# Two-layer hybrid decoder trunk: the opening's shift and scale columns side by side in one accumulator

## The chip, the cores and the metric
The kernel runs on one core of one Trainium2 chip. The metric is the device time of one execution in microseconds (us). Engines are named as in the profile: PE (TensorE, matrix products; PEld its weight loads), DVE (VectorE), ACT (ScalarE), POOL (GpSimd) and SP (SyncE, which issues most loads). Each engine works through its own list of instructions in order. SBUF is the on-chip memory, PSUM the eight banks that PE writes to.

## What is computed
Two decoder layers over 256 positions of width D = 2048 in float32. Each has a token mixer (layer 0 forgetting attention, layer 1 sliding-window attention) and a gated feed-forward network. Each of these four sub-layers is modulated by vectors made from one conditioning vector `c`:

```python
c_act = jax.nn.silu(c)
for i in range(DEPTH):
    mod = c_act @ ada_w[i] + ada_b[i]                 # ada_w[i]: 2048 x 12288
    sh1, sc1, g1, sh2, sc2, g2 = jnp.split(mod[:, None, :], 6, axis=-1)
    h = x * (1.0 + sc1) + sh1
    y = fox_attention(h, fox_w_in[j], ...)            # layer 0: proj = h @ w_in; layer 1: swa_attention
    x = layer_norm(DEEPNORM_ALPHA * x + (1.0 + g1) * y, ...)
    h = x * (1.0 + sc2) + sh2
    y = conv_ffn(h, ...)
    x = layer_norm(DEEPNORM_ALPHA * x + (1.0 + g2) * y, ...)
```

Nothing of layer 0 can start before `sh1` and `sc1` (the first 2 x 2048 columns of `ada_w[0]`, 33.6 MB) are at least partly known. The change concerns how these two vectors are made.

## The kernel before
Weights are used in two float32r halves: a load `w` (two blocks of 128 rows by 512 columns, 512 KB) is rounded by ACT to `wh` (L276, a cast) and DVE makes the residual `wl = w - wh` (L287). PE multiplies both with the modulated, transposed input `hHL` (`hH` high, `hL` low half). Matmuls into `ws` are query and key projections, into `xs` value projections.

The **opening** (`opening`, with `first_block` for the projections) works in eight chunks of 256 of the 2048 columns of `sh1` and `sc1`; the variable is `cb`, and the texts say chunk 0 to 7. For a chunk:

1. SP loads the `ada_w` columns into tiles `wo` (L531), each with 4 of the 16 blocks of 128 rows, for 256 columns of the shift (v = 0) or the scale (v = 1): 8 loads of 512 KB. All loads, `wo` and `w`, share ten buffers (`wp`); a load is issued when the tile that held its buffer has been used. Every second chunk also loads 512 columns of x (512 KB).
2. Each row block is multiplied by its constant of `c_act` (`cact`, one per partition) and summed in the accumulator `oacc`. Shift and scale have separate columns, and each has two accumulators for even and odd row blocks, so four per chunk. The first product of each goes to POOL (L541, a TENSOR_SCALAR), the others to DVE (L543, a SCALAR_TENSOR_TENSOR: multiply and add). In chunk 0, three of each eight row blocks go to PE instead (`cps<-cact,wo`).
3. PE sums over the partitions by a product with ones (`cps<-ones,oacc`, 8 matmuls). A float32 matmul shows as two records in the trace.
4. DVE adds the bias: `cv` (L573, one for shift, one for scale). PE transposes the chunk's part of x (`sm<-ident,x`, L469, 4 transposes in `mod_turn`). `mod_pair` makes `hHL` of it: ACT and DVE write one half each of `t` (L484, L485), ACT rounds it (L85), DVE subtracts (L86).

From chunk 1 on, six weight loads per chunk (two items of `plan`, each with query, key and value part) run through `first_block` between these steps, with the input columns that earlier chunks have finished. After a chunk pair, ACT scales its columns of x in place by a constant (L639, in `scaled`), which may not happen before x has been transposed. After the opening the rest of the projections, attention, and so on follow, with the weights streamed in the same way; there DVE makes the other modulation vectors in the same manner (L404, L406, 1024 columns at a time).

The program's text doesn't fix the order in which an engine's instructions stand: a scheduler orders them by its own estimate of when each can run, except those handed to `pin`, which stay in program order among themselves. Eight semaphores, used in turn, mark landed transfers of SP; a load is issued only when the load eight before it has landed.

Of the kernel before, what the change touches and what calls it, by code (L numbers as in the profile page):

```python
# [10 lines left out]
F32 = mybir.dt.float32  # L11
# [3 lines left out]
ALU = mybir.AluOpType  # L15
AX = mybir.AxisListType

P = 128
D = 2048
S = 256  # L20
NT = S // P
KC = D // P
# [19 lines left out]
def hybrid_trunk(ctx: ExitStack, tc: tile.TileContext, a: dict, out: bass.AP):  # L42
    nc = tc.nc
# [5 lines left out]
    cst = ctx.enter_context(tc.tile_pool(name="cst", bufs=1))  # L49
    wp = ctx.enter_context(tc.tile_pool(name="wp", bufs=10))  # L50
# [12 lines left out]
    def ttile(name="t"):  # L63
        return tp.tile([P, 2 * S], F32, tag="t", name=name)

    def bank(name="sm"):
        return psp.tile([P, 512], F32, tag="ps", name=name)
# [7 lines left out]
    def mm(o, lhsT, rhs, start=False, stop=False, **kw):  # L75
        return nc.tensor.matmul(o, lhsT, rhs, start=start, stop=stop, **kw)  # L76

    def pin(ins, on=True):

        if on:  # L80
            tc.keep_in_program_order(ins)

    def split(h, l, src):

        nc.scalar.copy(h, src)  # L85
        nc.vector.tensor_tensor(l, src, f32(h), op=ALU.subtract)  # L86
# [16 lines left out]
    ones = cst.tile([P, P], F32, name="ones")  # L103
# [19 lines left out]
    cact = cst.tile([P, KC], F32, name="cact")  # L123
# [3 lines left out]
    acol = cst.tile([P, DEPTH, NADA], F32, name="acol")  # L127
# [259 lines left out]
    cols = {}  # L387
# [74 lines left out]
    def mod_turn(k, n=1):  # L462

        ps = [bank() for _ in range(n)]
        os = []
        for j in range(2):
            o = ps[j % n][:, j // n * S:(j // n + 1) * S]
            for t in range(NT):
                nc.tensor.transpose(o[:, t * P:(t + 1) * P], x[:, t, (k + j) * P:(k + j + 1) * P], ident)  # L469
            os.append(o)  # L470
        return os

    def mod_pair(G, B, k, ps, fast=False):
        tmp = ttile()
        if fast:
            g, b = ([c[:, k + j:k + j + 1] for j in range(2)] for c in (G, B))
            o = [tmp[:, j * S:(j + 1) * S] for j in range(2)]
            high = lambda j: nc.scalar.activation(hH[:, k + j, :], ps[j], AF.Identity, bias=b[j], scale=g[j])
            whole = lambda j: pin(nc.vector.tensor_scalar(o[j], ps[j], g[j], b[j], op0=ALU.mult, op1=ALU.add))
            high(0), whole(1), high(1), whole(0)  # L480
            for j in range(2):
                pin(nc.vector.tensor_tensor(hL[:, k + j, :], o[j], f32(hH[:, k + j, :]), op=ALU.subtract))  # L482
            return
        nc.scalar.activation(tmp[:, :S], ps[0], AF.Identity, bias=B[:, k:k + 1], scale=G[:, k:k + 1])  # L484
        nc.vector.tensor_scalar(tmp[:, S:], ps[1], G[:, k + 1:k + 2], B[:, k + 1:k + 2],  # L485
                                op0=ALU.mult, op1=ALU.add)
        split(hH[:, k:k + 2, :], hL[:, k:k + 2, :], tmp.rearrange("p (j s) -> p j s", j=2))
# [6 lines left out]
    def warm(n):  # L494

        o = bank("warm").rearrange("p (a b) -> p a b", b=P)
        for _ in range(n):
            pin(mm(o, onesr, onesr.unsqueeze(1).broadcast_to([P, 4, P]), start=True, stop=True))
# [21 lines left out]
    def opening(plan, proj, also):  # L520

        CB = 2 * P
        QK = 1024 // CB
        for v in range(2):
            cols[0, v] = cst.tile([P, KC], F32, tag=f"cv{v}", name="cv")

        def sums(cb, v, acc, ps):
            pe = 8 - (3 if cb == 0 else 0)
            for kq in range(0, KC, QK):
                w = wp.tile([P, QK, CB], F32, tag="w", name="wo")  # L530
                nc.sync.dma_start(w, a["ada_w"][0, kq * P:(kq + QK) * P, v * D + cb * CB:v * D + (cb + 1) * CB]  # L531
                                  .rearrange("(k p) f -> p k f", p=P))
                for k in range(QK):
                    kc = kq + k
                    if kc % 8 >= pe:
                        for j in range(2):
                            c = 2 * v + j
                            mm(ps[:, c:c + 1], w[:, k, j * P:(j + 1) * P], cact[:, kc:kc + 1],
                               start=c == 0 and kc == pe, skip_group_check=True)
                    elif kc < 2:  # L540
                        nc.gpsimd.tensor_scalar_mul(acc[:, v, k % 2, :], w[:, k, :], cact[:, kc:kc + 1])  # L541
                    else:
                        nc.vector.scalar_tensor_tensor(acc[:, v, k % 2, :], w[:, k, :], cact[:, kc:kc + 1],  # L543
                                                       acc[:, v, k % 2, :], op0=ALU.mult, op1=ALU.add)
                yield

        accs = cst.tile([P, D], F32, tag="acc", name="oacc").rearrange("p (c v q f) -> p c v q f", c=2, v=2, q=2)
        for cb, items in enumerate(plan):
            k = 2 * cb
            todo = [(*it, part) for it in items for part in range(3)]  # L550
            n = len(todo)
            if cb == D // CB:
                for it in todo:
                    proj(*it)
                break
            acc = accs[:, cb % 2]
            ps = bank("cps")
            also.get(cb, lambda: None)()
            steps = [g for v in range(2) for g in [sums(cb, v, acc, ps)] * (KC // QK)]
            for i, g in enumerate(steps):  # L560
                if i == 0 and cb % 2 == 0:
                    c = slice(cb * CB, (cb + 2) * CB)
                    nc.sync.dma_start(x[:, :, c], a["x"][0][:, c].rearrange("(t p) d -> p t d", p=P))
                next(g)
                while todo and n - len(todo) < (i + 1) * n // len(steps):
                    proj(*todo.pop(0))
            for c in range(4):
                for q in range(2):
                    mm(ps[:, c:c + 1], acc[:, c // 2, q, c % 2 * P:(c % 2 + 1) * P], ones[:, 0:1],
                       start=cb > 0 and c == q == 0, stop=q == 1, skip_group_check=True)  # L570
            tps = mod_turn(k)
            for v in range(2):
                nc.vector.scalar_tensor_tensor(cols[0, v][:, k:k + 2], ps[:, 2 * v:2 * v + 2], float(v),  # L573
                                               acol[:, 0, v * KC + k:v * KC + k + 2], op0=ALU.add, op1=ALU.add)
            mod_pair(cols[0, 1], cols[0, 0], k, tps)


    stats = cst.tile([P, NT, D // 512, nc.vector.BN_STATS_DIM], F32, name="stats")
# [152 lines left out]
    def fox(l, j):  # L731
# [128 lines left out]
        def first_block(blk, k2, part):  # L860
# [24 lines left out]
            done[blk] = k + 2  # L885

        opening(plan, first_block, {6: forget_load})
        settle()
        forget_split()
# [222 lines left out]
    for t in range(NT):  # L1112
        mu, rs, _ = moments[t]
        for d in range(D // 512):
            c = slice(d * 512, (d + 1) * 512)
# [29 lines left out]
```

## Time and profile before

| | us |
|---|---|
| median of 3 runs | 2278.4 (2278.16 to 2280.16) |
| profiled execution, its own time | 2278.65 |
| its span in the trace | 2276.9 |
| last `cv` of the opening (chunk 7) | 185.33 |
| DVE multiply-adds of the opening (L543) | 212, together 92.5 busy |
| POOL products of the opening (L541) | 32, together 43.6 busy |

The profile's page gives busy times and shares, and the costliest groups of instructions. Its other views: stretches of time (busy time of each engine between two moments), the table of waits (who waited for whom, in total), and the timeline, in which a row gives start, duration, engine, line, operation, output<-inputs, shapes, count, and in brackets how long the engine stood idle before and what ended that.

### The profile page before, as it was taken

What the parts mean: (1) busy time and instruction counts of PE and PEld (TensorE: products, weight loads), DVE (VectorE), ACT (ScalarE), POOL (GpSimd) and SP (SyncE); (2) the same over time, 40 slices, a digit from 0 to 9 for tenths busy, and PEclk for the clock granted to TensorE, in tenths of its full rate; (3) what the DMA queues carried; (4) which work ended last, traced back from release to release, by engine and by line L of the source; (5) the groups of instructions that cost most, each with busy time, mean ns of one, the idle gap of its engine ahead of it and who ended that gap; (6) DMA issues with size and microseconds to landing.
All of it is one profiled execution on the core that took longest, in us unless ns stands there. A gap on an engine that the chain in (4) does not pass through costs nothing. (4 is left out here: it accounts for less than half of the span.)

```text
span 2276.9 us, 33423 instructions
## 1 busy us (share of the span) xinstructions
PE 2216.4 (97%) x12225; PEld 1902.6 (84%) x12225; DVE 1864.8 (82%) x2783; ACT 1183.8 (52%) x1859; POOL 63.8 (3%) x83
## 2 busy tenths in 40 slices
PE   7889999999999999999999999999999999999997
PEld 7789898778888888888888788778888888888886
DVE  6888999979988978878888989889988655666766
ACT  3335644446655533555534488746555533555542
POOL 3230000000000000000000000000000000000000
PEclk9999999999999999999999999999999999999999
DMA  9998999868987889878888776778887556666553
GB/s 346 330 327 291 352 348 357 319 239 295 325 273 235 292 323 323 287 241 271 290 296 287 260 257 207 237 250 289 285 270 249 183 194 194 187 193 192 187 194 111
DMA packets 285988, 602.66 MB, mean 265 GB/s; under 512 B 20790, under 2 KB 53752, under 8 KB 285312
## 3 DMA queue, kind: packets, MB, share of 16 engines
q1 hardware_dynamic: 284768, 595.85, 77.6%
q0 software_dynamic: 1056, 4.69, 0.6%
q8 instruction: 95, 1.56, 0.3%
q14 instruction: 69, 0.57, 0.1%
HBM read 598.37 MB, written 2.10 MB: 264 GB/s over the span
## 5 line engine op out<-in xcount | busy, mean ns | idle before, releaser
L276 ACT CAST wh<-w 128x1024 fp32r<-128x1024 f32 x728 | 762.8, 1051 | 759.9 <-PE xs L76 285.8
L287 DVE TENSOR_TENSOR wl<-w,wh 128x1024 fp32r<-128x1024 f32 x728 | 886.3, 1220 | 299.6 <-ACT wh L276 270.2
L76 PE MATMUL wd<-hHL,wh 128*128 128x512 f32 x2816 | 717.9, 397 | 1.1 <-DVE hHL L482 1.1
L76 PEld LDWEIGHTS wd<-hHL,wh 128*128 128x128 f32 x2816 | 503.5, 188 | 100.1 <-issue 2.9
L76 PEld LDWEIGHTS wd<-hHL,wl 128*128 128x128 f32 x2816 | 373.3, 188 | 32.8 <-DVE wl L287 1.6
L76 PE MATMUL wd<-hHL,wl 128*128 128x256 f32 x2816 | 379.6, 277 | 1.1 <-DVE wl L287 1.1
L406 DVE SCALAR_TENSOR_TENSOR acc<-wa,cact,acc 128x1024 f32<-128x1024 f32 x300 | 380.1, 1276 | 0.0
L76 PE MATMUL xs<-wh,gT 128*128 128x512 f32 x1408 | 349.7, 390 | 0.0
L76 PEld LDWEIGHTS xs<-wh,gT 128*128 128x128 f32 x1408 | 263.5, 188 | 54.2
L76 PE MATMUL xs<-wl,gT 128*128 128x512 f32 x704 | 189.3, 389 | 0.0
L76 PE MATMUL xs<-wh,hHL 128*128 128x512 f32 x704 | 185.8, 401 | 2.8 <-DVE hHL L86 2.7
L76 PEld LDWEIGHTS xs<-wl,gT 128*128 128x128 f32 x704 | 132.2, 188 | 27.6
L76 PEld LDWEIGHTS xs<-wh,hHL 128*128 128x128 f32 x704 | 129.0, 190 | 29.5 <-DVE hHL L86 3.5
L76 PE MATMUL ws<-hHL,wh 128*128 128x256 f32 x1024 | 136.8, 287 | 16.1 <-ACT wh L276 16.1
L76 PEld LDWEIGHTS ws<-hHL,wh 128*128 128x128 f32 x1024 | 127.3, 194 | 21.8 <-ACT wh L276 21.3
L1035 ACT ACTIVATE u<-s,ccol 128x256 f32<-128x256 f32 x176 | 104.6, 599 | 66.4 <-DVE s L1030 48.7
L76 PE MATMUL xs<-wl,hHL 128*128 128x512 f32 x352 | 98.5, 400 | 1.5 <-DVE wl L287 1.3
L76 PE MATMUL xs<-wh,oT 128*128 128x512 f32 x384 | 98.8, 395 | 0.1
L543 DVE SCALAR_TENSOR_TENSOR oacc<-wo,cact,oacc 128x256 f32<-128x256 f32 x212 | 92.5, 495 | 6.4 <-POOL oacc L541 6.3
L1036 DVE SCALAR_TENSOR_TENSOR u<-s,ccol,u 128x255 f32<-128x255 f32 x176 | 83.8, 477 | 5.7 <-ACT u L1035 5.6
L1038 DVE SCALAR_TENSOR_TENSOR u<-s,ccol,u 128x254 f32<-128x254 f32 x176 | 83.6, 476 | 1.1
L76 PEld LDWEIGHTS xs<-wh,oT 128*128 128x128 f32 x384 | 69.9, 188 | 13.9 <-ACT pT L688 0.6
(220 smaller groups left out, 1694.3 us busy)
## 6 DMA issues: line engine op xcount, KB each, us to landing
w<-in_ffn_w_up_dram SPq DMA_DIRECT2D x352, 512.0 KB, 4.6
wa<-in_ada_w_dram SPq DMA_DIRECT2D x320, 512.0 KB, 5.1
w<-in_ffn_w_down_dram SPq DMA_DIRECT2D x176, 512.0 KB, 4.3
w<-in_fox_w_in_dram SPq DMA_DIRECT2D x96, 512.0 KB, 5.6
wo<-in_ada_w_dram SPq DMA_DIRECT2D x64, 512.0 KB, 6.5
w<-in_swa_w_in_dram SPq DMA_DIRECT2D x40, 512.0 KB, 5.5
w<-in_fox_w_o_dram SPq DMA_DIRECT2D x32, 512.0 KB, 6.0
w<-in_swa_w_o_dram SPq DMA_DIRECT2D x32, 512.0 KB, 5.3
```

What stands on the lines that cost most here:

```text
L76: return nc.tensor.matmul(o, lhsT, rhs, start=start, stop=stop, **kw)
L276: pin(nc.scalar.copy(h, w), False)
L287: pin(nc.vector.tensor_tensor(l, w, f32(h), op=ALU.subtract), go in behind)
L406: pin(nc.vector.scalar_tensor_tensor(ac, wo, cact[:, k:k + 1], ac, op0=ALU.mult, op1=ALU.add), True)
L543: nc.vector.scalar_tensor_tensor(acc[:, v, k % 2, :], w[:, k, :], cact[:, kc:kc + 1], acc[:, v, k % 2, :], op0=ALU.mult, op1=ALU.add)
L1035: nc.scalar.activation(u, s, AF.Identity, bias=cw(CW, f), scale=cw(2, f))
L1036: nc.vector.scalar_tensor_tensor(u[:, 1:], s[:, :S - 1], cw(1, f), u[:, 1:], op0=ALU.mult, op1=ALU.add)
L1038: nc.vector.scalar_tensor_tensor(u[:, 2:], s[:, :S - 2], cw(0, f), u[:, 2:], op0=ALU.mult, op1=ALU.add)
```

## The change
Shift and scale columns of a row block are now loaded side by side, into a tile of 2 row blocks x (256 shift + 256 scale) columns; each row block is a load of its own (256 KB), two to a tile. One multiply-add covers the 512 columns, into one accumulator per chunk. POOL makes one product of 512 columns per chunk (row block 0). In chunk 0 PE takes only row block 10. The sums over partitions are 4 matmuls. The accumulators of four chunks have places of their own (before: two). In chunk 0 PE also gets 6 and 8 matmuls on a constant whose result nobody uses (`warm`), the transposes go to two banks, and `mod_pair` takes its other form, in which ACT writes `hH` straight from PSUM (L478) and DVE works on one column block at a time. One multiply-add of chunk 1 is tied behind chunk 0's `cv`.

```diff
@@ def opening(plan, proj, also):
-        QK = 1024 // CB
+        QK = 512 // CB
-        def sums(cb, v, acc, ps):
-            pe = 8 - (3 if cb == 0 else 0)
+        def sums(cb, acc, ps):
             for kq in range(0, KC, QK):
-                w = wp.tile([P, QK, CB], F32, tag="w", name="wo")
-                nc.sync.dma_start(w, a["ada_w"][0, kq * P:(kq + QK) * P, v * D + cb * CB:v * D + (cb + 1) * CB]
-                                  .rearrange("(k p) f -> p k f", p=P))
+                w = wp.tile([P, QK, 2, CB], F32, tag="w", name="wo")
                 for k in range(QK):
                     kc = kq + k
-                    if kc % 8 >= pe:
-                        for j in range(2):
-                            c = 2 * v + j
-                            mm(ps[:, c:c + 1], w[:, k, j * P:(j + 1) * P], cact[:, kc:kc + 1],
-                               start=c == 0 and kc == pe, skip_group_check=True)
-                    elif kc < 2:
-                        nc.gpsimd.tensor_scalar_mul(acc[:, v, k % 2, :], w[:, k, :], cact[:, kc:kc + 1])
+                    nc.sync.dma_start(w[:, k], a["ada_w"][0, kc * P:(kc + 1) * P, :2 * D]
+                                      .rearrange("p (v d) -> p v d", v=2)[:, :, cb * CB:(cb + 1) * CB])
+                for k in range(QK):
+                    kc = kq + k
+                    wk = w[:, k].rearrange("p v f -> p (v f)")
+                    if cb == 0 and kc == 10:
+                        for c in range(4):
+                            pin(mm(ps[:, c:c + 1], wk[:, c * P:(c + 1) * P], cact[:, kc:kc + 1], start=c == 0, skip_group_check=True))
+                        warm(6)
+                    elif kc == 0:
+                        nc.gpsimd.tensor_scalar_mul(acc, wk, cact[:, kc:kc + 1])
+                    elif cb == 1 and kc == 1:
+                        with tc.issue_after(first_cv[0].ins):
+                            nc.vector.scalar_tensor_tensor(acc, wk, cact[:, kc:kc + 1], acc, op0=ALU.mult, op1=ALU.add)
                     else:
-                        nc.vector.scalar_tensor_tensor(acc[:, v, k % 2, :], w[:, k, :], cact[:, kc:kc + 1],
-                                                       acc[:, v, k % 2, :], op0=ALU.mult, op1=ALU.add)
+                        nc.vector.scalar_tensor_tensor(acc, wk, cact[:, kc:kc + 1], acc, op0=ALU.mult, op1=ALU.add)
                 yield
...
-            acc = accs[:, cb % 2]
+            acc = accs[:, cb % 4]
...
             for c in range(4):
-                for q in range(2):
-                    mm(ps[:, c:c + 1], acc[:, c // 2, q, c % 2 * P:(c % 2 + 1) * P], ones[:, 0:1],
-                       start=cb > 0 and c == q == 0, stop=q == 1, skip_group_check=True)
-            tps = mod_turn(k)
+                pin(mm(ps[:, c:c + 1], acc[:, c * P:(c + 1) * P], ones[:, 0:1], start=cb > 0 and c == 0, stop=True,
+                       skip_group_check=True), cb == 0)
+            if cb == 0:
+                warm(8)
+            tps = mod_turn(k, 2 if cb == 0 else 1)
...
-            mod_pair(cols[0, 1], cols[0, 0], k, tps)
+            mod_pair(cols[0, 1], cols[0, 0], k, tps, cb == 0)
```

The scheduler also puts other instructions of the opening in another order. In the rows below, a name is a tile, its shape follows, and xN is the number of such instructions in a row. On DVE, the whole of chunk 2 from the `cv` of chunk 1 to its own, before:

```order
L573 SCALAR_TENSOR_TENSOR cv<-cps,acol 128x2 x2
L287 TENSOR_TENSOR wl<-w,wh 128x1024
L485 TENSOR_SCALAR t<-sm,cv 128x256
L543 SCALAR_TENSOR_TENSOR oacc<-wo,cact,oacc 128x256
L86 TENSOR_TENSOR hHL<-t,hHL 128x2x256
L543 SCALAR_TENSOR_TENSOR oacc<-wo,cact,oacc 128x256 x5
L287 TENSOR_TENSOR wl<-w,wh 128x1024
L543 SCALAR_TENSOR_TENSOR oacc<-wo,cact,oacc 128x256 x4
```

The chunk goes on with residuals `wl` and groups of 4, 6, 4 and 4 multiply-adds, 28 in all. The same place on DVE now (line numbers have moved by 4 to 6), to the end of the chunk:

```order
L578 SCALAR_TENSOR_TENSOR cv<-cps,acol 128x2 x2
L287 TENSOR_TENSOR wl<-w,wh 128x1024
L485 TENSOR_SCALAR t<-sm,cv 128x256
L547 SCALAR_TENSOR_TENSOR oacc<-wo,cact,oacc 128x512
L86 TENSOR_TENSOR hHL<-t,hHL 128x2x256
L547 SCALAR_TENSOR_TENSOR oacc<-wo,cact,oacc 128x512 x3
L287 TENSOR_TENSOR wl<-w,wh 128x1024
L547 SCALAR_TENSOR_TENSOR oacc<-wo,cact,oacc 128x512 x2
L287 TENSOR_TENSOR wl<-w,wh 128x1024
L547 SCALAR_TENSOR_TENSOR oacc<-wo,cact,oacc 128x512 x2
L287 TENSOR_TENSOR wl<-w,wh 128x1024
```

It ends with groups of 4, 2 and 1, each behind a residual but the last `cv`: 15 multiply-adds, each of which waits for the one before it on the same accumulator; the first waits for POOL.

On ACT, from the `t` of chunk 2 to that of chunk 3, before:

```order
L484 ACTIVATE t<-sm,cv 128x256
L85 CAST hHL<-t 128x2x256
L276 CAST wh<-w 128x1024 x3
L639 ACTIVATE x<-x 128x2x512
L276 CAST wh<-w 128x1024 x3
L484 ACTIVATE t<-sm,cv 128x256
```

And now, with the scaling of x (L645, before L639) moved behind the `t` of chunk 3:

```order
L484 ACTIVATE t<-sm,cv 128x256
L85 CAST hHL<-t 128x2x256
L276 CAST wh<-w 128x1024 x6
L484 ACTIVATE t<-sm,cv 128x256
L645 ACTIVATE x<-x 128x2x512
L85 CAST hHL<-t 128x2x256
```

The six casts stand together. On PE, chunk 3 from the partition sums of the first half, before:

```order
L76 MATMUL cps<-ones,oacc 128x1 x4
L469 MATMUL sm<-ident,x 128x128 x3
L76 MATMUL xs<-wh,hHL 128x512 x8
L76 MATMUL xs<-wl,hHL 128x512 x4
L469 MATMUL sm<-ident,x 128x128
L76 MATMUL ws<-hHL,wh 128x256 x16
```

And now, at the end of chunk 3, where all four sums and all four transposes stand between two halves of the residual matmuls (in chunks 1, 2 and 4 they stand behind all eight, ahead of the next 16 `wh` matmuls):

```order
L76 MATMUL ws<-hHL,wh 128x256 x16
L76 MATMUL ws<-hHL,wl 128x256 x4
L76 MATMUL cps<-ones,oacc 128x1 x4
L469 MATMUL sm<-ident,x 128x128 x4
L76 MATMUL ws<-hHL,wl 128x256 x4
L76 MATMUL xs<-wh,hHL 128x512 x8
```

No transpose is left behind the value matmuls. Behind the opening, PE's and ACT's rows are the same in both kernels.

More of the change, by code (lines that the diff above doesn't have):

```diff
@@ L545, in sums @@
                 yield
-        accs = cst.tile([P, D], F32, tag="acc", name="oacc").rearrange("p (c v q f) -> p c v q f", c=2, v=2, q=2)
+        first_cv = []
+        accs = cst.tile([P, D], F32, tag="acc", name="oacc").rearrange("p (c a) -> p c a", a=2 * CB)
         for cb, items in enumerate(plan):
@@ L555, in opening @@
                 break
-            acc = accs[:, cb % 2]
+            acc = accs[:, cb % 4]
             ps = bank("cps")
             also.get(cb, lambda: None)()
-            steps = [g for v in range(2) for g in [sums(cb, v, acc, ps)] * (KC // QK)]
+            steps = [sums(cb, acc, ps)] * (KC // QK)
             for i, g in enumerate(steps):
@@ L567, in opening @@
             for c in range(4):
-                for q in range(2):
-                    mm(ps[:, c:c + 1], acc[:, c // 2, q, c % 2 * P:(c % 2 + 1) * P], ones[:, 0:1],
-                       start=cb > 0 and c == q == 0, stop=q == 1, skip_group_check=True)
-            tps = mod_turn(k)
+                pin(mm(ps[:, c:c + 1], acc[:, c * P:(c + 1) * P], ones[:, 0:1], start=cb > 0 and c == 0, stop=True,
[3 more added lines that the diff above has]
+            tps = mod_turn(k, 2 if cb == 0 else 1)
             for v in range(2):
-                nc.vector.scalar_tensor_tensor(cols[0, v][:, k:k + 2], ps[:, 2 * v:2 * v + 2], float(v),
-                                               acol[:, 0, v * KC + k:v * KC + k + 2], op0=ALU.add, op1=ALU.add)
-            mod_pair(cols[0, 1], cols[0, 0], k, tps)
+                first_cv[:] = [nc.vector.scalar_tensor_tensor(cols[0, v][:, k:k + 2], ps[:, 2 * v:2 * v + 2], float(v),
+                                                              acol[:, 0, v * KC + k:v * KC + k + 2],
+                                                              op0=ALU.add, op1=ALU.add)]
+            mod_pair(cols[0, 1], cols[0, 0], k, tps, cb == 0)
     stats = cst.tile([P, NT, D // 512, nc.vector.BN_STATS_DIM], F32, name="stats")
```

## The prediction
> **What bounds the kernel now.** I read the page first: PE is busy 97% of the span, so only idle PE time can be won. The slices show where it lies: at the start. I then cut the opening at its eight `cv` instructions on DVE (L573, one pair per chunk), because each closes a chunk. In the view by stretches the columns are start:end, length, busy time (instructions) of PE, PEld, DVE, ACT and POOL, granted clock, DMA share, GB/s:
> ```profile
> span 2276.9 us, 33423 instructions
> PE 2216.4 (97%) x12225; PEld 1902.6 (84%) x12225; DVE 1864.8 (82%) x2783; ACT 1183.8 (52%) x1859; POOL 63.8 (3%) x83
> 0.00:23.98 23.98, 15.15 (x70) 14.83 (x70) 7.56 (x20) 1.59 (x2) 9.99 (x26) 1.00 0.93 319
> 23.98:46.10 22.12, 17.84 (x126) 17.00 (x127) 18.95 (x37) 11.16 (x15) 6.37 (x4) 1.00 1.07 387
> 46.10:68.11 22.01, 19.67 (x141) 17.73 (x141) 20.10 (x39) 10.10 (x14) 6.05 (x4) 1.00 1.00 343
> 68.11:93.18 25.07, 21.82 (x144) 19.76 (x144) 19.85 (x38) 7.92 (x9) 4.97 (x4) 0.93 1.00 340
> 93.18:115.09 21.91, 19.32 (x138) 17.39 (x138) 19.73 (x39) 10.10 (x14) 4.70 (x4) 1.00 0.92 304
> 115.09:140.12 25.03, 22.22 (x144) 19.95 (x144) 19.99 (x38) 7.93 (x9) 6.90 (x4) 0.93 0.95 290
> 140.12:161.91 21.79, 19.96 (x141) 18.00 (x141) 20.00 (x38) 7.29 (x8) 5.75 (x4) 1.00 1.03 361
> 161.91:185.33 23.42, 20.14 (x141) 17.92 (x141) 19.63 (x39) 7.93 (x9) 5.62 (x7) 1.00 0.99 334
> 300.00:400.00 100.00, 99.93 (x655) 90.75 (x654) 92.54 (x114) 46.55 (x78) 0.00 (x0) 1.00 0.97 359
> ```
> From 300 us on PE has no gap, and its order behind the opening is the same in both kernels, so what the opening saves, the kernel saves. In the opening no engine is full: a chunk takes 22 to 25 us, with DVE busy for 20 of them. What holds it together is in the table of waits (first two rows: the SP queue's own; waited in all, times, longest):
> ```profile
> SPq L273 <- DVE oacc L543: 52.4, 39, 3.9
> SPq L531 <- DVE oacc L543: 47.6, 40, 2.6
> DVE cv L573 <- PE cps L76: 16.0, 8, 3.9
> DVE wl L287 <- ACT wh L276: 9.0, 5, 2.7
> ```
> The loads wait 100 us for DVE to free a tile: DVE sets the pace, and the transfers, at up to 387 GB/s, follow. DVE itself waits for PE's column sums (16.0) and for ACT's casts (9.0). The second is mostly one stall that comes three times, in chunks 3, 5 and 7 (the timeline of several engines; in brackets the idle time before, and who ended it):
> ```profile
> 82.56 0.27 PE L469 MATMUL sm<-ident,x 128*128 128x128 f32 x1
> 82.87 1.06 ACT L639 ACTIVATE x<-x 128x1024 f32<-128x1024 f32 x1 [9.44 <-PE sm L469]
> 84.89 1.23 DVE L287 TENSOR_TENSOR wl<-w,wh 128x1024 fp32r<-128x1024 f32 x1 [2.69 <-ACT wh L276]
> 131.88 1.23 DVE L287 TENSOR_TENSOR wl<-w,wh 128x1024 fp32r<-128x1024 f32 x1 [2.69 <-ACT wh L276]
> 178.70 1.23 DVE L287 TENSOR_TENSOR wl<-w,wh 128x1024 fp32r<-128x1024 f32 x1 [2.69 <-ACT wh L276]
> 84.91 3.38 PE L76 MATMUL ws<-hHL,wh 128*128 128x256 f32 x16 [2.08 <-ACT wh L276]
> 107.54 2.10 PE L76 MATMUL ws<-hHL,wh 128*128 128x256 f32 x16 [1.16 <-ACT wh L276]
> ```
> ACT's scaling of x (L639) stands ahead of three weight casts and waits 9.44 us for the last transpose, which PE runs only at 82.56. Casts, DVE and PE all stand behind it, and PE then runs at 3.38 us for what takes 2.10 after a shorter gap.
>
> **The multiply-adds.** 212 of 256 columns become 119 of 512 (14 in chunk 0, 15 in each other), and each waits for the one before, since there is one accumulator. Nearest prices:
> ```profile
> 73.18 1.22 DVE L287 TENSOR_TENSOR wl<-w,wh 128x1024 fp32r<-128x1024 f32 x1
> 74.31 1.66 DVE L543 SCALAR_TENSOR_TENSOR oacc<-wo,cact,oacc 128x256 f32<-128x256 f32 x4
> 2260.71 1.40 DVE L1116 SCALAR_TENSOR_TENSOR x<-x,mv,ln 128x512 f32<-128x512 f32 x2
> 2262.03 1.41 DVE L1117 SCALAR_TENSOR_TENSOR x<-x,rs,ln 128x512 f32<-128x512 f32 x2
> 2263.36 0.74 DVE L1116 SCALAR_TENSOR_TENSOR x<-x,mv,ln 128x512 f32<-128x512 f32 x1
> 2053.42 0.48 DVE L1036 SCALAR_TENSOR_TENSOR u<-s,ccol,u 128x255 f32<-128x255 f32 x1
> 2053.93 0.48 DVE L1038 SCALAR_TENSOR_TENSOR u<-s,ccol,u 128x254 f32<-128x254 f32 x1
> ```
> Start to start, independent 256-column ones go at (1.66 - 0.48)/3 = 0.395 us; 512-column ones at (2262.03 - 2260.71)/2 = 0.66. The last two rows are a dependent pair: 0.51 apart, 0.115 more than independent ones. So a dependent 512-column one costs 0.66 + 0.115 = 0.775. In a chunk 8 of the 15 stand directly behind their predecessor, and 7 have another instruction between: 8 x 0.775 + 7 x 0.66 = 10.8 us against 28 x 0.395 = 11.1. The gain by instruction count is nearly eaten by the chain: 0.3 us per chunk.
> By the Trainium skill ("VectorE: DVE Perf Modes", The DRAIN you can't avoid) a semaphore between Vector instructions "costs nothing extra here"; the pair above disagrees (0.51 against 0.395). By the skill's rule all 15 would go at 0.66, 9.9 us, and the forecast below would fall by another 0.9 x 7 = 6.3 us.
>
> **POOL's products**: 4 of 256 columns per chunk become 1 of 512, half the columns. Where POOL works, DVE slows:
> ```profile
> 29.48 2.03 DVE L543 SCALAR_TENSOR_TENSOR oacc<-wo,cact,oacc 128x256 f32<-128x256 f32 x4
> 28.30 3.38 POOL L541 TENSOR_SCALAR oacc<-wo,cact 128x256 f32<-128x256 f32 x2 [7.17 <-DMA wo<-in_ada_w_dram]
> 40.36 2.99 POOL L541 TENSOR_SCALAR oacc<-wo,cact 128x256 f32<-128x256 f32 x2 [8.67 <-DMA wo<-in_ada_w_dram]
> 46.10 0.23 DVE L573 SCALAR_TENSOR_TENSOR cv<-cps,acol 128x2 f32<-128x2 f32 x2 [1.75 <-PE cps L76]
> ```
> 2.03 against 1.66, 0.37 more, twice a chunk; one of the two goes: 0.4 us, between 0 (the same columns moved elsewhere) and 0.7. The new product is awaited by the whole chain. Chunk 2's pair of two was done at 43.35, 2.75 us before the `cv` behind which DVE needs it; that cover hides it, and if the first tile came 3 us later it would show.
>
> **Column sums**: 8 per chunk become 4, in one place. DVE waited 1.75 us for them at the end of chunk 1. Half the matmuls take this to about 1.2: 0.5 us saved. Bounds: 0.9 saved (half of all of it), or 1 us lost where PE is behind, since DVE's multiply-adds are queued behind `cv`. In chunks 1, 2 and 4 the sums now stand ahead of 16 matmuls whose weights are ready; From the residual `wl` just ahead to the last multiply-add DVE needs 0.66 + 0.775 + 1.13 (a residual's start to start, 73.18 to 74.31) + 0.74 = 3.3 us; PE fills 1.1 of them:
> ```profile
> 62.50 1.07 PE L76 MATMUL ws<-hHL,wl 128*128 128x256 f32 x8
> ```
> So it idles 2.2 us, and then may run 1.3 us slow (3.38 - 2.10). Chunk 2 has PE busy 19.67 of 22.01, so it can bear this once the chunk is not much under 21.
> **ACT's scaling** now stands behind `t` of its own chunk, and the four transposes together ahead of the last residual matmuls; the six casts no longer wait. The 2.69 us stall goes in chunks 3, 5 and 7. Late next there: the same DVE chain.
>
> **Chunk 0**:
> ```profile
> 8.04 0.93 POOL L541 TENSOR_SCALAR oacc<-wo,cact 128x256 f32<-128x256 f32 x1 [5.08 <-DMA wo<-in_ada_w_dram]
> 12.85 7.68 PE L76 MATMUL cps<-cact,wo 128*128 128x1 f32 x36
> 20.39 3.55 PE L76 MATMUL cps<-ones,oacc 128*128 128x1 f32 x16
> ```
> Before, PE's column products and sums end it at 23.94. Now half the first tile suffices to start POOL, some 0.8 us earlier (estimate: 256 KB less at 319 GB/s), which takes 1.85 for 512 columns (2 x 0.93): 9.1. Then 14 x 0.775 = 10.9 on DVE, 20.0; sums 3.55/2 = 1.8: `cv` at about 22, 2 us earlier. The 14 warming matmuls lie in PE's idle time but for the last 8, which delay the transposes by 2 to 3.5 us; DVE has three multiply-adds of the next chunk (2.2 us) meanwhile.
> **Loads**: 64 of 512 KB become 128 of 256 KB, the same bytes in the same 1 KB runs:
> ```profile
> w<-in_fox_w_in_dram SPq DMA_DIRECT2D x96, 512.0 KB, 5.6
> wo<-in_ada_w_dram SPq DMA_DIRECT2D x64, 512.0 KB, 6.5
> ```
> A chunk loads 8 + 6 pieces of 512 KB (the latter weights of three-part blocks) and on average half a 512 KB piece of x: 7.6 MB, 19.6 us at the 387 GB/s of chunk 1. That is the floor. The split adds 64 issues on SP, which waited 100 us over the same 64 and some 42 weight loads; at the 0.37 us of one issue,
> ```profile
> 60.53 0.37 SPq L273 DMA_DIRECT2D w<-in_fox_w_in_dram  x1
> ```
> they take 24 us out of that wait. I cost them at nothing, with the wait as cover; without it they would be up to 3 us a chunk.
>
> **The sum.** Chunk 2 is undisturbed: 22.01 - 0.3 - 0.4 - 0.5 = 20.8. Bounds are 19.6 (transfers) and 23 (nothing gained, the PE wait lost). With PE's new gap and the close floor I take 21.2. Seven chunks: 148.4, on 22.0: the last `cv` at 170.4 instead of 185.33, 14.9 us earlier. Span 2276.9 gives 2262.0. The profiled execution took 2278.65 and the runs' median is 2278.4, so 2263.5.
>
> **Rivals.**
> 1. The chain of 15 and PE's gap eat all but the ACT stall and chunk 0: chunks stay at 22.0. For it: the even price (10.8 against 11.1). Against: three separate terms fall. 22.0 + 7 x 22.0 = 176.0, 9 us earlier: 2269.
> 2. The transfers alone bound it: chunks of 19.6, last `cv` at 22.0 + 7 x 19.6 = 159.2, 26 us earlier: 2252. For it: chunk 1 at 387 GB/s. Against: DVE busy 20.1 in chunk 2, and my terms take the chunk, waits included, to 20.8 and no lower. The skill's rule on the chain, above, would bring this about; the dependent pair speaks against it.
> 3. Slower: 256 KB loads move less per second. Through the last `cv` 64 + 42 + 4 pieces of 512 KB must come (products, weights, x), 57.7 MB, the first some 5 us after the start, so below 57.7/(185.3 - 5) = 320 GB/s the opening is longer than now. At the 290 of chunk 5 it ends at 5 + 199 = 204: 19 us later, 2297. For it: the rows' mean is 334 GB/s, little above 320. Against: the low rates go with SP waiting for DVE, not with full queues.
> This is also the Trainium skill's rule ("DMA: Bandwidth & Descriptors", Bandwidth): batch transfers to 1 MiB or more, smaller ones reach less of peak. No row here shows 256 KB loads in flow, so the trace does not decide it.
> 4. No change: every slot saved is given back at `cv` and the ACT order does not matter; 2274 to 2283, about 2279.
>
> **How the numbers follow.** Within 0.2% (4.6 us) is about what a measurement of this kernel cannot tell from no change. My forecast, chunks of 20.4 to 21.9, 2258 to 2268.5: 0.55. Rival 1, up to 2273.5: 0.17. Rival 2: 0.13. Rival 3: 0.07. Rival 4: 0.08. The range takes the forecast, rival 1 and the nearer half of rival 2: 2255 to 2273.5. Faster 0.86, same 0.07, slower 0.07.
>
> **What would show it.** Right: the last `cv` near 170; chunks 3, 5, 7 no longer than 2 and 4; no wait of ACT's x scaling over 2 us; dependent 512-column multiply-adds 0.77 apart; DVE still near full between `cv`s. Wrong: GB/s lower with SP not waiting for DVE (rival 3), or `cv` waiting over 3 us for PE in most chunks (rival 1 or 4).

## The result, and the profile after

| | before | after |
|---|---|---|
| median of the runs (13 each) | 2278.96 us (2278.16 to 2281.46) | 2273.26 us (2270.82 to 2275.08) |
| profiled execution | 2278.65 us | 2271.15 us |
| its span | 2276.9 us | 2269.4 us |
| last `cv` | 185.33 | 176.61 |

The ratio is 0.9971, 95% interval [0.9963, 0.998]: faster, but by 5.7 us where 15 were forecast. The changed kernel's profiled execution lies 2.1 us below its median, so the trace shows 7.5 of a gain whose median is 5.7.

The stretches between the `cv`s (now L578) after the change, in the columns of the same table of before:
```profile
0.00:25.16 25.16, 7.15 (x25) 5.79 (x26) 11.63 (x18) 1.59 (x2) 7.15 (x22) 1.00 0.94 322
25.16:48.76 23.60, 18.80 (x106) 16.39 (x107) 18.32 (x27) 9.91 (x14) 1.56 (x1) 0.93 1.00 339
48.76:71.85 23.09, 19.88 (x134) 18.36 (x133) 19.32 (x26) 10.92 (x15) 2.04 (x1) 0.93 0.97 320
71.85:92.22 20.37, 20.37 (x154) 19.15 (x153) 18.85 (x26) 7.20 (x8) 2.88 (x1) 1.00 0.99 339
92.22:113.46 21.24, 16.61 (x114) 14.70 (x113) 19.36 (x25) 10.93 (x15) 2.19 (x2) 1.00 1.06 382
113.46:135.07 21.61, 21.61 (x154) 20.61 (x154) 18.83 (x25) 7.20 (x8) 2.31 (x1) 0.92 0.92 287
135.07:156.26 21.19, 18.69 (x134) 16.73 (x134) 18.93 (x25) 8.33 (x9) 1.14 (x1) 1.00 1.05 353
156.26:176.61 20.35, 18.64 (x134) 17.04 (x134) 18.83 (x25) 7.40 (x8) 2.99 (x6) 1.00 1.07 392
```
Chunks 3 to 7 take (176.61 - 71.85)/5 = 20.95 us on average, 21.2 were forecast. The first three miss the forecast: chunk 0 ends at 25.16, later than the 23.98 of before, and chunks 1 and 2 take 23.60 and 23.09, longer than before. What the last `cv` missed lies there.

Chunk 0 on DVE (timeline; in brackets the idle time before, and who ended it):
```profile
8.64 3.17 DVE L547 SCALAR_TENSOR_TENSOR oacc<-wo,cact,oacc 128x512 f32<-128x512 f32 x4 [4.95 <-POOL oacc L542]
14.60 0.18 DVE L176 TENSOR_SCALAR nsink<-sink 128x32 f32<-128x32 f32 x1 [2.79 <-DMA sink<-in_swa_sinks_dram]
...
15.07 8.13 DVE L547 SCALAR_TENSOR_TENSOR oacc<-wo,cact,oacc 128x512 f32<-128x512 f32 x10
25.16 0.23 DVE L578 SCALAR_TENSOR_TENSOR cv<-cps,acol 128x2 f32<-128x2 f32 x2 [1.96 <-PE cps L76]
```
`nsink`, 0.18 us of work on a small constant, stands in DVE's row between the fourth and the fifth multiply-add and waits 2.79 us for its load; ten multiply-adds queue behind it. The kernel before had the same wait (timeline of before):
```profile
15.84 0.18 DVE L176 TENSOR_SCALAR nsink<-sink 128x32 f32<-128x32 f32 x1 [2.89 <-DMA sink<-in_swa_sinks_dram]
16.55 3.50 DVE L543 SCALAR_TENSOR_TENSOR oacc<-wo,cact,oacc 128x256 f32<-128x256 f32 x8
```
There it cost nothing: DVE was done at 20.05 all the same, while PE was at its column products until 20.4 and then at the sums, which ended chunk 0.

Around the `cv` that closes chunk 0, on PE (timeline):
```profile
24.99 3.76 PE L76 MATMUL warm<-ones 128*128 128x512 f32 x8
28.55 0.97 PE L469 MATMUL sm<-ident,x 128*128 128x128 f32 x4
31.60 2.86 PE L76 MATMUL ws<-hHL,wh 128*128 128x256 f32 x16 [0.33 <-DVE hHL L482]
34.25 1.91 PE L76 MATMUL ws<-hHL,wl 128*128 128x256 f32 x8
```
The 8 warming matmuls hold the transposes until 28.55, and the matmuls behind are slow all the same (2.86 and 1.91 for what took 2.10 and 1.07 in the rows of before that the prediction shows).

Chunk 1 on ACT, and DVE's waits for it in chunks 1 and 2 (timeline of both engines):
```profile
41.02 1.07 ACT L886 COPY part<-xs 128x512 f32<-128x512 f32 x2 [1.44 <-PE xs L76]
41.98 2.96 ACT L276 CAST wh<-w 128x1024 fp32r<-128x1024 f32 x3
43.07 1.23 DVE L287 TENSOR_TENSOR wl<-w,wh 128x1024 fp32r<-128x1024 f32 x1 [1.00 <-ACT wh L276]
60.94 1.23 DVE L287 TENSOR_TENSOR wl<-w,wh 128x1024 fp32r<-128x1024 f32 x1 [1.54 <-ACT wh L276]
```
ACT's copies of finished tiles (`part`) stand in pairs ahead of the casts and wait for PE, and three casts queue behind the last pair. In chunks 1 and 2 DVE waits 0.90, 1.00, 1.54 and 0.67 us for casts. The kernel before had such copies too, but with a cast between the last two, and there DVE waited for a cast 0.72 us in chunk 1 and not at all in chunk 2.

SP's waits until the last `cv` (waited in all, times, longest):
```profile
SPq L532 <- DVE wl L287: 17.7, 15, 2.4
SPq L532 <- DMA wo<-in_ada_w_dram: 15.7, 51, 1.1
SPq L532 <- DVE oacc L547: 13.0, 17, 4.5
SPq L273 <- DMA w<-in_fox_w_in_dram: 12.3, 17, 1.7
```
A load now often waits for the landing of an earlier load (33 us with a further row of the view, 5.1 us in which L532 waits for a `w`), where before such waits came to 0.6 us. Whether that is a new bound is what the experiments had to tell apart from the three places above.

### The profile page after: what moved, and what is told of

The parts are those of the page before. It is cut to its first block, busy times and chain, and to the rows that moved or that the text cites. A ratio compares the mean times of both kernels' runs of the same rounds, so it can differ in the third digit from the quotient of the medians.

```text
span 2269.4 us, 33231 instructions
## 1 busy us (share of the span) xinstructions
PE 2202.8 (97%) x12135; PEld 1889.6 (83%) x12135; DVE 1863.2 (82%) x2692; ACT 1184.0 (52%) x1859; POOL 35.7 (2%) x59
## 5 line engine op out<-in xcount | busy, mean ns | idle before, releaser
L547 DVE SCALAR_TENSOR_TENSOR oacc<-wo,cact,oacc 128x512 f32<-128x512 f32 x118 | 89.5, 759 | 7.3 <-POOL oacc L542 4.9
```

Of the source, the lines that this page charges most:

```text
L547: nc.vector.scalar_tensor_tensor(acc, wk, cact[:, kc:kc + 1], acc, op0=ALU.mult, op1=ALU.add)
```

## The experiments

The theory (A): chunk 0 lost its gain to `nsink`, chunk 1 to the warming matmuls, chunks 1 and 2 to ACT's order. The main rival (B): the 256 KB loads, waiting for landings, set the pace, so whatever is mended comes back as a wait for transfers. Runs 1 and 3 also have a third reading, called C in both, though it is another one in each. Each run's ratio is against the kernel before. Where two runs differ by less than their intervals, the text goes by the `cv`s of the profile; a profile is a single execution, and its time lies up to 2.4 us from the median of its run.

**1. One thing of the change alone.** The kernel before, with ACT's scaling of x behind the `t` of its own odd chunk:
```
+        t_act.append(nc.scalar.activation(tmp[:, :S], ps[0], ...))
...
+            with tc.issue_after(t_act[2 * d + 1].ins):
-            nc.scalar.mul(x[...], x[...], ALPHA)
+                nc.scalar.mul(x[...], x[...], ALPHA)
```


> The kernel before, with one thing of the change alone: ACT's scaling of x (L639) is tied behind the t of its own odd chunk, so that no weight cast stands behind it. Theory A (most of what the change gained is this stall of 2.69 us, three times, with PE's slow matmuls behind it): chunks 3, 5 and 7 fall from 25.07, 25.03 and 23.42 to about 22, the last cv from 185.3 to about 178, the time to about 2271.5, which is what the whole change reached. Rival C (the side-by-side columns brought the gain, and the stall would only be replaced by another wait): the chunks stay over 24 and the time within 2 us of 2279.

Measured: 2270.56 us against 2280.3, ratio 0.9959 [0.9946, 0.9971]. Its chunks 3, 5 and 7 in the view by stretches:
```profile
68.31:89.33 21.02, 19.86 (x144) 18.07 (x144) 19.90 (x38) 7.08 (x8) 6.07 (x4) 1.00 0.98 336
111.50:132.53 21.03, 19.87 (x144) 18.07 (x144) 19.54 (x38) 7.19 (x8) 4.64 (x4) 1.00 0.93 281
154.38:175.42 21.04, 19.68 (x141) 17.86 (x141) 19.55 (x39) 7.30 (x8) 5.51 (x7) 1.00 1.06 398
```
They were 25.07, 25.03 and 23.42. One instruction of each odd chunk, moved on ACT, gives as much as the whole change (0.9959 against 0.9971, intervals that overlap); C (the columns brought the gain) falls. All the rest of the change together, columns, loads, warming and new orders, was worth nothing net: its last `cv` is at 176.61, here at 175.42. By stage: the change loses 71.85 - 68.31 = 3.5 us in chunks 0 to 2 and gains 2.35 us, 0.47 a chunk, in chunks 3 to 7.

**2. `nsink` and `posf` out of chunk 0.** In the changed kernel:
```
+        with tc.issue_after(first_cv[-1].ins):
-        nc.vector.tensor_scalar_mul(nsink, sink, -1.0)
-        nc.vector.tensor_copy(posf, posr)
+            nc.vector.tensor_scalar_mul(nsink, sink, -1.0)
+            nc.vector.tensor_copy(posf, posr)
```


> The changed kernel, with the two small DVE instructions nsink (L176) and posf (L178) tied behind the cv of chunk 0 instead of standing behind the fourth multiply-add. Theory A (chunk 0 is DVE's chain, and the 2.8 us that nsink waits for the load of sink is paid in full): the cv of chunk 0 moves from 25.16 to about 22.4, the last cv from 176.6 to about 174, the time falls by 2 to 3 us against the changed kernel. Theory B (the 256 KB loads, each waiting for the landing of the one eight before, pace the opening: SP waits 36 us for landings): chunk 0's cv is earlier, chunk 1 is longer by the same, the last cv stays within 0.7 us of 176.6 and the time within 1 us.

The two ran behind the last `cv` in fact, since the list held that one by then; for chunk 0 that is the same. Measured: 2269.42 us, 0.9955 [0.9942, 0.9967]; last `cv` 174.67. DVE's timeline in chunk 0, then the first two stretches:
```profile
8.71 11.33 DVE L550 SCALAR_TENSOR_TENSOR oacc<-wo,cact,oacc 128x512 f32<-128x512 f32 x14 [4.89 <-POOL oacc L545]
```
```profile
0.00:22.00 22.00, 7.12 (x25) 5.79 (x26) 11.30 (x17) 1.59 (x2) 7.58 (x22) 1.00 0.93 317
22.00:46.73 24.73, 20.23 (x106) 17.65 (x107) 18.62 (x27) 9.92 (x14) 1.62 (x1) 1.00 1.05 373
```
The fourteen multiply-adds run as one chain, and chunk 0 ends at 22.00, as forecast. Chunk 1 takes back 1.1 of the 3.2 us. The warming matmuls and ACT's order are still there; runs 4 and 6 take them out one after the other, and chunk 1 falls to 21.67 and then to 19.49.

**3. No warming matmuls** (`warm(6)` and `warm(8)` taken out; the transposes then come before the sums).


> The changed kernel without the 6 and the 8 warming matmuls of chunk 0. The four transposes then stand in front of the column sums, and the first weights are split in two instructions ahead of the casts. Theory A (the last 8 warming matmuls hold up the transposes by 3.8 us, and with them chunk 1's first residuals, while PE's matmuls are slow at 31.6 anyway, 2.86 us for 16): t comes 3 to 4 us earlier, chunk 1 shrinks from 23.6 to about 21.5, the last cv moves by about -2. Theory B (transfers pace the opening): chunk 1 stays at 23 or more and the last cv within 0.7 us of 176.6. Theory C (the warming does what it is there for): the first matmuls of chunk 1 run slow for longer (over 3.4 us for 16) and the time rises by 1 us or more.

Measured: 2269.7 us, 0.9955 [0.9943, 0.9968]; last `cv` 173.79. Chunk 1 falls to 20.53, further than theory A had it (21.5), but chunk 2 grows from 23.09 to 24.29, at a granted clock of 0.88. The first matmuls of chunk 1 (PE's timeline):
```profile
27.75 3.42 PE L76 MATMUL ws<-hHL,wh 128*128 128x256 f32 x16 [3.02 <-ACT wh L276]
31.00 1.07 PE L76 MATMUL ws<-hHL,wl 128*128 128x256 f32 x8
```
Without warming 16 + 8 matmuls take 4.5 us in all, with it 2.86 + 1.91 = 4.8, and they start 3.85 us earlier. (The granted clock of the rows does not show this slow start: by them it was 1.00 here until 36 us.) The condition of C, that the warming does what it is there for, was met by 0.02 us (3.42 for the 16), but its consequence, a longer time, did not come.

**4. Both.**


> Both edits before together: nsink and posf behind the cv of chunk 0, no warming matmuls. Theory A: the terms add, last cv at 171 to 173, time 4 to 6 us below the changed kernel, so about 2268. Theory B (transfers): less than 1.5 us below it.

Measured: 2268.11 us, 0.9947 [0.9933, 0.996]; last `cv` 172.92, chunks 22.23, 21.67, 23.05, 21.61, and so on. The time is as theory A had it. At the last `cv` the two gains of 1.9 and 2.8 us come to 3.7 together, not to the full 4.8. Chunk 2 stays long.

**5. ACT's copies behind the casts**, in the changed kernel:
```
-            pin(nc.scalar.copy(h, w), False)
+            last_cast[:] = [nc.scalar.copy(h, w)]
...
+                        with tc.issue_after(last_cast[0].ins):
-                        nc.scalar.copy(g, ...)
+                            nc.scalar.copy(g, ...)
```


> The changed kernel, with ACT's copies of finished projection tiles (L886) tied behind the latest weight cast, so that in chunks 1, 2 and 4 each pair of copies stands one cast later in ACT's row than now. Theory A (chunks 1 and 2 are long because casts stand behind copies that wait for PE: DVE waits 0.90, 1.00, 1.54 and 0.67 us for casts in them): these waits go, chunks 1 and 2 fall from 23.6 and 23.1 to about 22 each, the last cv from 176.6 to about 174, the time by 1.5 to 2.5 us. Theory B (transfers pace these chunks): the waits turn into waits of the casts for the loads and the last cv stays within 0.7 us of 176.6.

Measured: 2270.93 us, 0.9963 [0.9951, 0.9976]. The median is 2.3 us below the changed kernel's, as theory A had it, but the intervals overlap; in the profiled execution, the slowest of the five, the last `cv` is at 176.64, as theory B had it. Yet in it chunks 1 and 2 did what theory A said (stretches of chunks 1, 2, 3 and 5, then PE's timeline ahead of chunk 3):
```profile
25.29:46.79 21.50, 18.20 (x106) 16.27 (x107) 18.57 (x26) 9.91 (x14) 1.57 (x1) 0.92 1.00 335
46.79:68.32 21.53, 19.39 (x133) 18.04 (x132) 19.15 (x26) 10.94 (x15) 1.66 (x1) 0.95 1.07 389
68.32:90.52 22.20, 22.20 (x154) 21.22 (x154) 18.92 (x25) 7.20 (x8) 3.05 (x1) 0.90 0.99 327
111.92:134.88 22.96, 22.96 (x154) 21.94 (x154) 19.36 (x25) 7.19 (x8) 2.07 (x1) 0.88 0.96 299
```
```profile
66.44 1.84 PE L76 MATMUL cps<-ones,oacc 128*128 128x1 f32 x8 [2.14 <-DVE oacc L548]
68.89 3.76 PE L76 MATMUL ws<-hHL,wh 128*128 128x256 f32 x16
```
What they gained, chunks 3 and 5 lost, and not to transfers: PE is busy in them throughout, at a granted clock of 0.90 and 0.88. Ahead of the sums PE idles 2.14 us, and behind them 16 matmuls take 3.76 us instead of 2.10. This is the gap at the column sums that the forecast priced at up to 1.3 us; here it costs the 16 matmuls 1.7. Neither theory had it as the next limit.

**6. All three edits.**


> nsink and posf behind chunk 0's cv, no warming matmuls, and ACT's copies behind the latest cast, all on the changed kernel. With the first two alone the last cv was at 172.9 and the time 2268.1; chunk 2 was still 23.05 long. Theory A: chunk 2 falls to 21.5, the last cv to about 171, the time to about 2266.5. Theory B (something else makes chunk 2 long, PE's gap at the column sums or the transfers): chunk 2 stays at 23 and the time at 2268.

Measured: 2264.34 us, 0.9934 [0.9921, 0.9946]; last `cv` 169.56; chunk 0 ends at 21.84. Chunks 1 to 3:
```profile
21.84:41.33 19.49, 14.80 (x94) 14.15 (x95) 18.04 (x27) 10.23 (x14) 2.48 (x1) 1.00 1.07 393
41.33:62.85 21.52, 19.06 (x133) 17.71 (x133) 19.14 (x26) 11.32 (x15) 2.11 (x2) 0.96 1.07 393
62.85:85.25 22.40, 22.40 (x154) 21.42 (x154) 19.14 (x26) 7.19 (x8) 2.23 (x1) 0.89 1.04 369
```
With the three places mended, the first three chunks end at 62.85 instead of 71.85, 9.0 us earlier, and the time is within 1 us of what was forecast for the change itself, though not chunk by chunk (19.49 and 22.40 us where 21.2 stood). Chunk 1 runs at 19.49 us and 393 GB/s, so it was not the 256 KB loads that held the changed kernel's chunks at 21 us and more: B falls for the change. Chunk 2 fell as theory A said, and chunk 3 took part of it back: PE is busy throughout at a clock of 0.89, 22.40 us for 154 matmuls that take 20.37 at 1.00 in chunk 3 of the changed kernel.

**7. Half loads alone.** The kernel before, each 512 KB load of `wo` as two of 256 KB:
```
-                nc.sync.dma_start(w, a["ada_w"][0, kq * P:(kq + QK) * P, ...])
+                for h in range(0, QK, 2):
+                    nc.sync.dma_start(w[:, h:h + 2], a["ada_w"][0, (kq + h) * P:(kq + h + 2) * P, ...])
```


> The kernel before, with each 512 KB load of modulation weights (L531) split into two loads of 256 KB, nothing else. It takes the number and size of the changed kernel's loads by itself. Theory A (256 KB loads cost nothing while SP waits 100 us for tiles anyway): chunks and time within 2 us of 2279, SP's wait for landings rises from under 1 us to tens and its wait for DVE falls by as much. Rival 3 of the forecast (256 KB loads move less a second): chunks longer, time over 2284.

Measured: 2278.45 us, ratio 0.9996 [0.9987, 1.0005]: nothing. SP's largest wait for DVE, and its largest for landings (all of these come to 15.6 us):
```profile
SPq L533 <- DVE oacc L545: 39.5, 38, 2.4
SPq L533 <- DMA wo<-in_ada_w_dram: 9.0, 28, 1.6
```
The waits for landings came with the number of loads, and they cost nothing here, where SP waits for tiles as well.

**8. Two accumulators** in turn, in the changed kernel (even and odd row blocks, so that no multiply-add reads what the last one wrote):
```
-                    elif kc == 0:
-                        nc.gpsimd.tensor_scalar_mul(acc, wk, cact[:, kc:kc + 1])
+                    elif kc < 2:
+                        nc.gpsimd.tensor_scalar_mul(acc[:, k], wk, cact[:, kc:kc + 1])
...
+                for q in range(2):
+                    pin(mm(ps[:, c:c + 1], acc[:, q, c * P:(c + 1) * P], ones[:, 0:1], ..., stop=q == 1, ...))
```


> The changed kernel with two accumulators in turn (even and odd row blocks, each 512 columns), so that no multiply-add reads what the one just before it wrote; POOL makes two products of 512 columns a chunk, DVE 14 multiply-adds, and PE sums both accumulators (8 matmuls again). Theory A (a dependent multiply-add costs 0.79 start to start where an independent one costs 0.66, about 8 times a chunk, and DVE's chain sets the pace): the multiply-adds go 0.66 apart, chunks 3 to 7 shrink by 0.8 to 1.5 us each with one multiply-add fewer as well, less 0.3 for the longer sums, the last cv at 169 to 173. Theory B (with loads that wait 36 us for landings the transfers are next in line): the multiply-adds go 0.66 apart but DVE waits more, chunks 3 to 7 stay within 0.4 us of 20.95 and the time within 1.5 us of the changed kernel's.

Measured: 2266.14 us, 0.9942 [0.9929, 0.9954]; last `cv` 173.35. On DVE, in chunks 2 and 6 (timeline):
```profile
60.30 2.73 DVE L547 SCALAR_TENSOR_TENSOR oacc<-wo,cact,oacc 128x512 f32<-128x512 f32 x4
149.22 0.75 DVE L547 SCALAR_TENSOR_TENSOR oacc<-wo,cact,oacc 128x512 f32<-128x512 f32 x1 [1.27 <-DMA wo<-in_ada_w_dram]
```
Four take 2.73 us, (2.73 - 0.74)/3 = 0.66 apart; in the changed kernel four took 3.11, 0.79 apart. Chunks 3 to 7 average 20.48 (20.95). Chunks 3, 5 and 7 go at 19.5 to 19.6, but chunk 6 takes 22.16, with two waits of DVE for loads in it (0.40 and 1.27 us), as theory B had it. The chunks shrink by 0.47, between the two theories (0.8 to 1.5 and under 0.4), and the last `cv` just misses A's 169 to 173. The median falls by 7.1 us, more than the 3.3 of the last `cv` (the profiled execution is the slowest of the five), and not by the chain alone: the column sums also lie otherwise on PE, most of them behind part of the next 16 matmuls, and PE keeps a clock of 1.00 from chunk 2 on. How much each brought is not separated.

**9. The scaling behind the cast of t.** Behind the last `cv` the changed kernel gives back 1 us: its first matmuls on a newly cast weight come 7.7 us earlier than before (181.08 against 188.79), its `cv` 8.7. On ACT there (timeline):
```profile
177.11 0.57 ACT L484 ACTIVATE t<-sm,cv 128x256 f32<-128x256 f32 x1 [2.42 <-PE sm L469]
177.57 1.05 ACT L645 ACTIVATE x<-x 128x1024 f32<-128x1024 f32 x1
178.52 1.04 ACT L276 CAST wh<-w 128x1024 fp32r<-128x1024 f32 x1
179.46 0.62 ACT L85 CAST hHL<-t 128x512 fp32r<-128x512 f32 x1
```
The run has the three edits of run 6, and the scaling tied behind the cast to `hHL` of its chunk.


> The three edits of the run before (nsink and posf late, no warming, copies behind casts), and ACT's scaling of x tied behind the cast of t to hHL (L85 in the changed kernel) in place of standing between t and that cast. In the changed kernel the last cv was 8.7 us earlier than before, the first matmul behind it only 7.7, and the span 7.5; ACT's rows there show the scaling, 1.05 us, ahead of the cast to hHL. Theory A (that 1 us is what was given back behind the opening, and it comes in chunks 2, 4 and 6 as well, where DVE waits about 0.7 us for the cast): the first matmul behind the last cv moves 1 us nearer to it, the time falls by 1 to 2.5 us from 2264.3 to 2262 to 2263.3. Rival B (what is given back lies in the softmax stage at 225 to 255 us, where PE waits 3 us for ACT and the granted clock falls to 0.89): the time stays within 0.5 us of 2264.3.

Measured: 2263.65 us, 0.9924 [0.991, 0.9937]. PE's matmuls behind the last `cv` (timeline), in run 6 and here:
```profile
174.03 2.31 PE L76 MATMUL ws<-hHL,wh 128*128 128x256 f32 x16 [0.44 <-ACT wh L280]
```
```profile
174.59 2.30 PE L76 MATMUL ws<-hHL,wh 128*128 128x256 f32 x18
```
The wait is gone, and the first score matmul (`S`, 208.10 and 208.73) comes 38.54 us behind the last `cv` there (169.56) and 37.68 here (171.05): 0.9 us nearer, as theory A said of this place. The other chunks did not shrink: in run 6 DVE waits for the cast to `hHL` only once, 0.7 us in all, and chunk 5 grew from 21.38 to 22.75, at clock 0.87. By the times the gain is not to be told from none.

**10. Everything.** Run 9 with two accumulators.


> The same with two accumulators in turn (two products of 512 columns on POOL, 14 independent multiply-adds on DVE, 8 column sums on PE). Theory A (with the stalls gone DVE's chain sets the pace again and the dependent step is 0.13 us, 8 times a chunk): chunks at 19.6 to 20.5, the last cv at 160 to 165, the time at 2256 to 2260. Rival B (the transfers are the bound at 19.6 to 21, and PE, which was late for the cv by 2.0 to 2.8 us in chunks 2 and 3 with these edits, takes back what DVE saves): last cv over 166, time over 2261.

Measured: 2258.0 us against 2280.28, ratio 0.9903 [0.9889, 0.9916]: the fastest, 22 us below the kernel before. Last `cv` 165.08. Chunks 1, 3, 5 and 6, and DVE's waits for loads in chunk 6 (waited in all, times, longest):
```profile
22.44:41.92 19.48, 17.03 (x116) 16.54 (x117) 16.93 (x26) 10.13 (x14) 2.92 (x2) 1.00 1.07 393
62.06:81.50 19.44, 19.44 (x146) 18.32 (x146) 17.37 (x24) 7.20 (x8) 4.89 (x3) 1.00 1.07 394
101.82:121.27 19.45, 19.45 (x146) 18.33 (x146) 17.36 (x25) 7.25 (x8) 2.13 (x3) 1.00 0.97 319
121.27:145.38 24.11, 20.27 (x141) 18.03 (x141) 17.98 (x25) 8.44 (x9) 2.79 (x3) 1.00 1.02 347
```
```profile
DVE oacc L554 <- DMA wo<-in_ada_w_dram: 3.4, 5, 1.1
```
The time is in theory A's range, the last `cv` 0.08 us beyond it. Chunk 1 is at the forecast's transfer floor, 19.5 us at 393 GB/s, with PE and DVE busy for 17 of them. Chunks 3 and 5 take as long, but there PE has no gap, and chunk 5 moves only 319 GB/s, so they do not show transfers as the limit. In chunk 6 DVE waits 3.4 us for loads, which come at 347 GB/s; why they come late there is not shown. Rival 2's bound is reached here at most in some chunks.

## Why the prediction was wrong

The direction was right, and so was most of the mechanism. The last `cv` came 6.2 us later than forecast (176.61 against 170.4): chunk 0 3.2, chunk 1 2.4, chunk 2 1.9, less 5 x 0.25 in chunks 3 to 7. Another 1.2 us were lost behind it, and 2.1 us is the distance of the profiled execution from the median.

- **Chunk 0, the step that failed first.** "14 x 0.775 = 10.9 on DVE" took the chain as whole. DVE's row has `nsink` and `posf` inside it, and they are in no term, though in the kernel before `nsink` waited 2.9 us for the same load. PE hid that wait then, and the change took this cover away. Run 2 gives the forecast 22.0, with 11.3 us for the 14.
- **The warming matmuls.** I had them delay the transposes by "2 to 3.5 us" with 2.2 us of multiply-adds as cover, and gave them no term in the sum. They delayed them by 3.6 (24.99 to 28.55), DVE stood idle for 1.93 us ahead of `t`, and everything of chunk 1 that hangs on `t` came late. Run 3: 2.8 us at the last `cv`.
- **ACT's order in chunks 1 and 2** was in no term of the sum: I had compared ACT's row in chunk 3 only, where there are no copies. Runs 4 and 6: with the copies behind the casts the last `cv` comes 3.4 us earlier. Alone (run 5) it moved nothing at the last `cv` of the profiled execution, since PE's slow clock took it.
- **The PE gap at the sums** was there, at about the forecast's 1.3 us. In the changed kernel PE idles 1.95 us ahead of the sums of chunk 4, the 16 matmuls behind take 2.96 us, and the `cv` that closes chunk 5 waits 2.46 us for PE instead of 1.21. In run 5 the 16 matmuls cost 1.7 more.
- **ACT's scaling**: right, and larger than I made it (chunks 3, 5 and 7 to 22.0, 7.5 us): in run 1 they go to 21.0, the last `cv` comes 9.9 us earlier, and this carries the whole measured gain. What I did not see is that its new place, between `t` and the cast to `hHL`, costs 0.9 us behind the last `cv`.
- **The multiply-adds**: right. Dependent 512-column ones go 0.79 apart (0.775 forecast), independent ones 0.66. The Trainium skill's sentence that a semaphore "costs nothing extra here" ("VectorE: DVE Perf Modes", The DRAIN you can't avoid), measured there on copies, does not hold for this chain.
- **Column sums**: right; DVE waits 1.21 us for them in six of eight chunks.
- **POOL's product**: its cover held; DVE waits for POOL in chunk 0 only. What its 0.4 us brought is not separated.
- **The size of the three terms per chunk**: 0.3, 0.4 and 0.5 us, taken as 0.8 with PE's gap. Against run 1, which has only the scaling, chunks 3 to 7 gained 0.47 each.
- **Loads costed at nothing**: right (run 7), and rival 3 did not come. The Trainium skill's rule on batching ("DMA: Bandwidth & Descriptors", Bandwidth) made no difference here: 256 KB loads, mixed with 512 KB ones, moved up to 394 GB/s.

The forecast's own range, 2258 to 2268.5, was missed. The median lies just inside the wider range's end, where rival 1 was put (up to 2273.5), but not for its reason: the chunks did not stay at 22.0, five of them went to 21 and three got worse. That the time came out in rival 1's place is luck.

## What to carry to other kernels

When a change shortens a chain that another engine used to hide, read every instruction that stands in the chain's own row, with its wait and not its work: a constant's 0.18 us can hold a queue for 2.8. Before an edit with many parts, try the one that removes the visible stall alone: here one moved instruction in every second chunk brought as much as the whole change. And where a list of instructions is ordered anew, look at each engine's row for work that now stands behind a wait.

## What the chip showed that I had not expected

- Eight warming matmuls of 512 columns (3.76 us) did not spare the slow start: 16 + 8 matmuls took 4.8 us behind them and 4.5 without. The granted clock fell to 0.50 at 32.7, after PE had idled 1.25 and 0.33 us behind the warming, and came back at 36.1.
- Idle time of 2.1 us ahead of the column sums is enough for slow matmuls behind them. In run 5 PE's last matmul ahead of the gap ended at 64.3 and the sums began at 66.44; cut into stretches of 0.1 us, the trace has the granted clock at 1.00 until 66.0 and at 0.50 from 66.1 to 72.8. So it fell after some 1.7 us of idle time, ahead of the sums, which were slow themselves (1.84 us, against 1.02 in chunks 1 to 4 of the changed kernel); the 16 matmuls took 3.76 us instead of 2.10. The Trainium skill ("TensorE: Matmul & The Clock Gate", Part 1: The HAM clock gate) puts the fall at an idle window of about 3.4 us. This trace does not agree with it: the whole gap was 2.14 us.
- The length of such a gap alone does not tell its price. In the changed kernel PE idles 1.57 us ahead of the sums at 47.70 and again at 70.79; the 16 matmuls behind them took 3.11 us the first time and 2.07 the second.
- Loads of 256 KB mixed with those of 512 KB moved 393 GB/s over whole chunks (runs 6 and 10), no less than the 387 that 512 KB loads alone reached before.
